# A two-layer decoder trunk: state-space tables with the channel innermost, another order of work around the last gate tile, and two rounds' banks exchanged

## The chip, the cores and the metric

One core of one Trainium2 chip runs the whole program. The metric is the device time of one execution in microseconds. Engines are named as in the profile: PE is TensorE, DVE VectorE, ACT ScalarE, POOL GpSimd, SP SyncE (which issues most transfers).

## The reference

Two layers over 512 tokens of 1024 channels. Each layer has a mixer, then a gated MLP with a causal convolution of width 3, then a gated per-layer embedding. The mixer of layer 0 is gMLP plus attention; that of layer 1 is a diagonal complex state-space layer (S5):

```python
bu_re = jnp.einsum('gpc,bsgc->bsgp', bb_re, uf)   # 64 groups of 16 channels, 64 states each
bu_im = jnp.einsum('gpc,bsgc->bsgp', bb_im, uf)
_, _, xr, xi = lax.associative_scan(_complex_affine_combine, (a_r, a_i, bu_re, bu_im), axis=1)
y = (jnp.einsum('gcp,bsgp->bsgc', c_re, xr) - jnp.einsum('gcp,bsgp->bsgc', c_im, xi) + d * uf)
g_a, g_b = jnp.split(jax.nn.gelu(y) @ od_w_glu, 2, axis=-1)
x = x + g_a * jax.nn.sigmoid(g_b)
# ends every layer:
gate = jax.nn.sigmoid(rms_norm(x) @ ple_w_gate[i])
x = x + gate * (p[i] @ ple_w_proj[i])
```

## The kernel before

Activations lie as 8 tiles of 128 channels x 512 tokens. Every large product is three matmuls (`mm3`): weights and activations are split into a high and a low half (`whi`, `wlo`), `whi` by ACT and `wlo` by DVE (class `Stream`: `prep` makes the halves of one 512 KB chunk, at most up to `limit`; `next` hands out a chunk). The program's order on each engine is the order of the code; small pieces are deferred with `after` (so many steps later) and `next_up`.

**The tables.** While the MLP of layer 0 runs, a generator, `s5_params`, makes the tables of the state-space layer in eight units of eight groups. It is advanced after each weight tile by `background`, which gives it a budget of microseconds per tile: `BG` = `up` for tiles of the up projection, `a` and `b` for the first and the last part of the down projection. A unit computes `ba` and `ca` on DVE (`cmul`, six instructions each), turns `ba` on PE (L1330) into `wv`, copies `bs` into `bd` on ACT (L1337), then multiplies `ca` by `bd` on PE (`kernel`, L1345) and copies `ca` into `wo` (`out_matrix`, L1357). What is left when the last part of the down projection has run seven steps is done at once (`embedding`).

**From the last gate to the first states.** `ple(0)` ends layer 0: eight gate tiles; each is scaled on DVE (L1034), goes through a sigmoid, and `add` puts it into `x[m]` (L1049, L1050). After `add`, `sq_add` squares the tile (ACT) and sums it (POOL, all but the last), and `s5_turn` writes it out turned (`xp`) so that `load_u` can read it as `u`. `state_space` then needs the norm (`rms_sum`, `rms_stat`, with a power on POOL, L213), spread by one small matmul (`scale`, L1486), and multiplies `u` with it (`scaled`, L1493). Eight projections of `p` (`p_proj`, six matmuls each) lie between these steps on PE.

**The state-space rounds.** Four rounds `b`, each of two units: `inputs` (V, L1507), `frame` (DVE and POOL: a rotation, two scans along time, L1522 and L1528, and the rotation back), `states` (four DVE adds into `sg`, L1542), `inside` (the part of a block of eight tokens, L1550, reads `tt`), `outside` (from the states, L1559, reads `wo`), `turn` (transposes), `done` (halves of the result, `ygl`). `part` is the first product of the following GLU. The numbers given to `inputs`, `inside`, `turn` and `bank` are PSUM banks: a step waits until the bank's last reader is through. The tiles `sg0` and `sg1` lie where the halves of `p` lay, so clearing their first column (L1620, POOL) waits for the last `p_proj`.

Of the kernel before, what the change touches and what calls it, by code (L numbers as in the profile page):

```python
# [19 lines left out]
P = 128  # L20
T = 512
# [133 lines left out]
class Kern:  # L155
# [709 lines left out]
    FA, FN, FO = 14, 7, 7  # L865
    BG = {"up": 1.1, "a": 3.3, "b": 2.4}

# [149 lines left out]
    def ple(self, layer, pl):  # L1017
# [11 lines left out]

        def gate(m, ps, c=slice(0, T)):  # L1030
            if c.start == 0:
                gt[m] = pl.tile([P, T], F32, name="gt", tag="gt", bufs=4)
            t = gt[m]
            nc.vector.tensor_tensor(t[:, c], ps[:, c], self.rB[:, c], ALU.mult)  # L1034

            def rest():
                nc.scalar.activation(t[:, c], t[:, c], AF.Sigmoid)
                if m and c.start == 0 and not (layer and m == KT - 1):
                    add(m - 1)
                if m == KT - 1 or (layer and m == KT - 2):  # L1040
                    add(m, c)

            self.post.append(rest)
            if m == KT - 1:
                self.run_post()

        def add(m, c=slice(0, T)):
            t = gt[m]
            nc.vector.tensor_tensor(t[:, c], t[:, c], pp[m][:, c], ALU.mult)  # L1049
            nc.vector.tensor_tensor(self.x[m][:, c], self.x[m][:, c], t[:, c], ALU.add)  # L1050
            if layer == 0:
                self.sq_add(m, self.x[m], m == KT - 1)
                self.s5_turn(m, pl)
            else:
                nc.sync.dma_start(self.out[m][:, c], self.x[m][:, c])
# [177 lines left out]
    def s5_params(self, g5):  # L1233
# [15 lines left out]
        for i in range(8):  # L1249
            q.tensor_copy(apr[:, :, :, i], ap[:, :, 7 - i])  # L1250
        apk = g5.tile([P, 2, 32, 9], F32, name="s5apk", tag="s5apk", bufs=1)
        for i in range(9):
            q.tensor_copy(apk[:, :, :, i], ap[:, :, i])
        v1, v2 = (g5.tile([P, 4, 144], F32, name=f"s5v{i}", tag=f"s5v{i}", bufs=1) for i in range(2))
# [48 lines left out]
        def unit(u):  # L1303
# [14 lines left out]

            ca = g5.tile([P, 2, 4, 16, 9], F32, name="s5ca", tag="s5ca", bufs=1)
            w = [v.rearrange("p a (c k) -> p a c k", c=16) for v in (v1, v2)]  # L1320
            ar, ai = (apk[:, r, g].rearrange("p g (o k) -> p g o k", o=1).to_broadcast([P, 4, 16, 9]) for r in range(2))
            cr, ci = (cc[:, r].rearrange("p g (c o) -> p g c o", o=1).to_broadcast([P, 4, 16, 9]) for r in range(2))
            yield from cmul(ca[:, 0], ca[:, 1], ar, ai, cr, ci, *w, 0.8)
# [16 lines left out]
            def kernel():  # L1340

                ps = self.aux()
                for i in range(4):
                    for r in range(2):
                        nc.tensor.matmul(ps[32 * i:32 * i + 32, 0:P], d[:, r, i],  # L1345
                                         ca[:, r, i, :, 0:8].rearrange("p c k -> p k c"), start=r == 0, stop=r == 1,
                                         tile_position=(0, 32 * i))
# [6 lines left out]
            def out_matrix():  # L1354
                wo = g5.tile([P, 2, 4, 128], F32, name="s5wo", tag="s5wv", bufs=1)
                for r in range(2):
                    nc.scalar.activation(wo[:, r].rearrange("p q (c i) -> p q c i", i=8), ca[:, r, :, :, 1:9], AF.Copy,  # L1357
                                         scale=1.0 - 2 * r)
# [14 lines left out]
    def s5_open(self, g5, s5a):  # L1373
# [3 lines left out]
        self.de = [s5a.tile([P, 8, 64], F32, name=f"de{i}") for i in range(4)]  # L1377
        self.m8 = g5.tile([P, 16, 8], F32, name="m8", tag="s5apk", bufs=1)
        self.nc.gpsimd.tensor_copy(self.m8, self.i8.rearrange("p (o i) -> p o i", o=1).to_broadcast([P, 16, 8]))
# [79 lines left out]
    def state_space(self, s5b):  # L1459
# [53 lines left out]
        def frame(b):  # L1513
# [9 lines left out]
            nc.gpsimd.tensor_tensor(t[5], t[1], si, ALU.mult)  # L1523
            nc.gpsimd.tensor_tensor(t[4], t[1], co, ALU.mult)
            tt(t[2], vi, co, ALU.mult)
# [18 lines left out]
        def inside(b, b0):  # L1544
# [3 lines left out]
            for g in range(8):  # L1548
                for k in range(2):
                    nc.tensor.matmul(Y[b][g // 4][64 * k:64 * k + 64, g % 4 * P:(g % 4 + 1) * P]  # L1550
                                     .rearrange("p (c i) -> p c i", i=8), self.ut[2 * b + k][:, g],
                                     tt[:, 8 * k + g].rearrange("p (i c) -> p c i", c=16), start=g % 4 == 0, stop=False)

        def outside(b):

            y = s5b.tile([P, 2, T], F32, name="y", tag="y", bufs=2)
            for g in range(8):
# [4 lines left out]
                if g % 4 == 3:  # L1562
                    nc.scalar.activation(y[:, g // 4], Y[b][g // 4], AF.Gelu_apprx_tanh)
            Y[b] = y

        def turn(b, b0):

            y = Y.pop(b).rearrange("p z (m i) -> p i (z m)", i=8)
            Z[b] = [bank(b0 + z, "Z") for z in range(2)]
# [34 lines left out]
        self.rms_sum(ps, self.sqa, True, False)  # L1604
        p_proj(w, 3, 7)
        self.rms_sum(ps, self.sql, False, True)
# [16 lines left out]
        p_proj(w, 7, 7)  # L1623
        self.load_in(4)
# [32 lines left out]
        inputs(3, 0, (1,))  # L1657
        frame(2)
        self.ws.dma(self.ws.n_use + 4)
        turn(1, 6)  # L1660
        inside(3, 2)
        done(1)
# [82 lines left out]
```

## Time and profile before

| | before |
|---|---|
| median of 3 runs | 1231.68 us (1229.73 to 1231.99) |
| profiled execution | 1233.72 us, its span 1232.0 us |
| granted PE clock, mean | 0.995 |
| PE / DVE / ACT / POOL busy | 98% / 64% / 43% / 22% |

The span is that of one profiled execution from its first to its last instruction; 1.7 us of its time lie around it. Busy shares are means over all stages. A PE that waits shows as a gap with the engine that ended it.

### The profile page before, as it was taken

Reading aid. Unit: us, or ns where it says so; the run is one execution under the profiler, and the core shown is the slowest. Engines: PE = TensorE matmul, PEld = TensorE weight load, DVE = VectorE, ACT = ScalarE, POOL = GpSimd, SP = SyncE. Lnnn points to the kernel's source line nnn. Section 1 sums busy time; section 2 is a strip of 40 time slices with the busy share of each in tenths; the row PEclk is TensorE's granted clock in tenths of the full one; section 3 lists DMA queues with packets and bytes.
Section 4 is the critical chain, followed back from the end, with each engine's and each line's share of the span. In section 5 each row is a group of like instructions: output and inputs, shape, how many; then the busy total and the mean of one; then the engine's idle time right before and its main releaser. Section 6 shows DMA issues by size and latency. Waiting matters only on the chain.

```text
span 1232.0 us, 15578 instructions
## 1 busy us (share of the span) xinstructions
PE 1208.4 (98%) x5858; PEld 973.0 (79%) x5858; DVE 784.5 (64%) x1156; ACT 531.8 (43%) x796; POOL 271.8 (22%) x453
## 2 busy tenths in 40 slices
PE   9999999999999999998999889999999999999998
PEld 7877678888888778886887678888888888888787
DVE  5597555599777866766545984538956532365545
ACT  5563664355444333444546124325544422234441
POOL 1561335870960221012402110110000000000110
PEclk9999999999999999999999999999999999999999
DMA  6323123233443554324487862332333233331441
GB/s 234 104 86 138 35 68 133 91 112 103 137 134 93 152 153 153 110 81 134 150 237 211 239 241 70 103 114 74 103 103 99 79 100 99 103 98 43 133 154 69
DMA packets 62314, 150.05 MB, mean 122 GB/s; under 512 B 14408, under 2 KB 23880, under 8 KB 62112
## 3 DMA queue, kind: packets, MB, share of 16 engines
q1 hardware_dynamic: 57504, 135.30, 35.5%
q0 software_dynamic: 4160, 12.90, 3.1%
q8 instruction: 46, 0.75, 0.3%
q10 hardware_dynamic: 576, 0.86, 0.2%
q14 instruction: 28, 0.23, 0.1%
HBM read 131.20 MB, written 17.84 MB: 121 GB/s over the span
## 4 chain that ended last, share of the span: by engine, by line
PE 91%; DVE 5%; DMA 1%; ACT 1%; issue 1%; SPq 0%; POOL 0%; ACTq 0%; DVEq 0%; POOLq 0%
PE acc L188 25%; PE acc L190 25%; PE acc L189 25%; PE acc L439 2%; PE acc L441 2%; PE acc L440 2%; PE S L721 1%; PE S L720 1%; PE m L779 1%; PE PT L762 1%; PE aux L1345 1%; PE fil L188 1%; PE fil L190 1%; DVE sg L1542 1%; PE fil L189 1%
## 5 line engine op out<-in xcount | busy, mean ns | idle before, releaser
L140 DVE TENSOR_TENSOR wlo<-raw,whi 128x1024 fp32r<-128x1024 f32 (+3 forms) x207 | 250.8, 1213 | 241.6 <-ACT whi L136 238.1
L136 ACT ACTIVATE whi<-raw 128x1024 fp32r<-128x1024 f32 (+3 forms) x207 | 208.9, 1010 | 358.5 <-PE acc L189 299.6
L188 PE MATMUL acc<-nl,whi 128*128 128x512 f32 x480 | 187.2, 390 | 0.0
L189 PE MATMUL acc<-nh,whi 128*128 128x512 f32 x480 | 186.8, 389 | 0.0
L190 PE MATMUL acc<-nh,wlo 128*128 128x512 f32 x480 | 186.8, 389 | 0.0
L241 POOL TENSOR_TENSOR sqa<-sqa,sqt 128x512 f32<-128x512 f32 x30 | 39.5, 1318 | 497.1 <-ACT sqt L237 497.1
L188 PE MATMUL acc<-xl,whi 128*128 128x512 f32 (+1 forms) x360 | 141.5, 393 | 0.0
L189 PE MATMUL acc<-xh,whi 128*128 128x512 f32 (+1 forms) x360 | 140.8, 391 | 0.0
L190 PE MATMUL acc<-xh,wlo 128*128 128x512 f32 (+1 forms) x360 | 140.8, 391 | 0.0
L188 PE MATMUL acc<-al,whi 128*128 128x512 f32 x352 | 139.8, 397 | 0.9 <-ACT whi L136 0.9
L190 PE MATMUL acc<-ah,wlo 128*128 128x512 f32 x352 | 138.3, 393 | 1.1 <-DVE wlo L140 1.1
L189 PE MATMUL acc<-ah,whi 128*128 128x512 f32 x352 | 138.3, 393 | 0.0
L188 PEld LDWEIGHTS acc<-nl,whi 128*128 128x128 f32 x480 | 90.1, 188 | 19.5 <-ACT whi L136 0.4
L190 PEld LDWEIGHTS acc<-nh,wlo 128*128 128x128 f32 x480 | 90.1, 188 | 18.8
L189 PEld LDWEIGHTS acc<-nh,whi 128*128 128x128 f32 x480 | 90.1, 188 | 18.6
L925 DVE SCALAR_TENSOR_TENSOR cv<-acc,vecs,cv 128x511 f32<-128x511 f32 x120 | 89.4, 745 | 2.1
L188 PEld LDWEIGHTS acc<-al,whi 128*128 128x128 f32 x352 | 66.3, 188 | 18.1 <-issue 2.6
L190 PEld LDWEIGHTS acc<-xh,wlo 128*128 128x128 f32 x360 | 67.8, 188 | 15.8
L189 PEld LDWEIGHTS acc<-xh,whi 128*128 128x128 f32 x360 | 67.8, 188 | 15.5
L188 PEld LDWEIGHTS acc<-xl,whi 128*128 128x128 f32 x360 | 67.8, 188 | 15.4
L190 PEld LDWEIGHTS acc<-ah,wlo 128*128 128x128 f32 x352 | 66.4, 189 | 16.7 <-DVE wlo L140 1.9
L189 PEld LDWEIGHTS acc<-ah,whi 128*128 128x128 f32 x352 | 66.5, 189 | 14.2
(386 smaller groups left out, 1974.5 us busy)
## 6 DMA issues: line engine op xcount, KB each, us to landing
raw<-w_up SPq DMA_DIRECT2D x88, 512.0 KB, 3.5
raw<-w_down SPq DMA_DIRECT2D x26, 512.0 KB, 3.5
raw<-w_in SPq DMA_DIRECT2D x19, 512.0 KB, 3.6
raw<-w_down SPq DMA_DIRECT2D x22, 384.0 KB, 3.1
raw<-w_gate SPq DMA_DIRECT2D x16, 512.0 KB, 3.6
raw<-w_glu SPq DMA_DIRECT2D x16, 512.0 KB, 4.3
x<-xT SPq DMA_DIRECT2D x16, 256.0 KB, 4.6
raw<-w_out SPq DMA_DIRECT2D x8, 512.0 KB, 3.6
```

The source lines that it names most:

```text
L136: k.nc.scalar.activation(hi[:, :n], t[:, :n], AF.Copy)
L140: e.tensor_tensor(lo[:, :n], t[:, :n], hi[:, :n].bitcast(F32), ALU.subtract)
L188: mm(out, whi, xlo, start=start, stop=False)
L189: mm(out, whi, xhi, start=False, stop=False)
L190: mm(out, wlo, xhi, start=False, stop=stop)
L241: (e or (nc.vector if m == KT - 1 else nc.gpsimd)).tensor_tensor(self.sqa, self.sqa, t, ALU.add)
L439: mm(ps[t], xl[:, ts], hi[:, cs], start=k == 0, stop=False)
L440: mm(ps[t], xh[:, ts], hi[:, cs], start=False, stop=False)
L441: mm(ps[t], xh[:, ts], lo[:, cs], start=False, stop=k == KT - 1)
L720: mm(ss[qi][:, 0:n], q[:, qs], k[:, 0:n], start=True, stop=False)
L721: mm(ss[qi][:, 0:n], q[rows, qs], kl[rows, 0:n], start=False, stop=True)
L925: nc.vector.scalar_tensor_tensor(t[:, k:T], h[:, 0:T - k], w[2 - k], t[:, k:T], ALU.mult, ALU.add)
```

## The change

1. `ca` is built as (k, c) instead of (c, k), straight from `ap`; the copy `apk` goes. The `kernel` matmul, the matmul of `inside` and the transposes then read along memory; `wo`, and the result tile `y`, have the token of the block outside and the channel inside.
2. The budgets of the generator: `up` from 1.1 to 1.3, `a` from 3.3 to 3.4.
3. In layer 0 `add(6)` is called ahead of the last gate's scaling, and tile 6's turned copy behind tile 7's square.
4. In `state_space` the two sums of the norm stand together, `p_proj(3)` behind them, `scale` at once behind that, `inputs(0)` behind `p_proj(4)`, `p_proj(7)` behind `inside(0)`. Weight chunks of the GLU are prepared only after `scaled(4..7)`.
5. In `frame`, one of the two POOL products goes to DVE.
6. The banks of `inputs(2)` and `inside(2)` change places, and so on for round 3; `inside(2)` and `turn(0)` go ahead of `inputs(2)`, and `inputs(3)` is no longer in two pieces.

```diff
-    BG = {"up": 1.1, "a": 3.3, "b": 2.4}
+    BG = {"up": 1.3, "a": 3.4, "b": 2.4}
...
+            last = layer == 0 and m == KT - 1
...
+            if last:
+                add(m - 1)
             t = gt[m]
             nc.vector.tensor_tensor(t[:, c], ps[:, c], self.rB[:, c], ALU.mult)
...
-                if m and c.start == 0 and not (layer and m == KT - 1):
+                if 0 < m < KT - 1 and c.start == 0:
                     add(m - 1)
...
+                if m == KT - 1:
+                    self.s5_turn(m - 1, pl)
                 self.sq_add(m, self.x[m], m == KT - 1)
-                self.s5_turn(m, pl)
+                if m != KT - 2:
+                    self.s5_turn(m, pl)
...
-            ca = g5.tile([P, 2, 4, 16, 9], F32, name="s5ca", tag="s5ca", bufs=1)
...
-            ar, ai = (apk[:, r, g].rearrange("p g (o k) -> p g o k", o=1).to_broadcast([P, 4, 16, 9]) for r in range(2))
-            cr, ci = (cc[:, r].rearrange("p g (c o) -> p g c o", o=1).to_broadcast([P, 4, 16, 9]) for r in range(2))
+            ca = g5.tile([P, 2, 4, 9, 16], F32, name="s5ca", tag="s5ca", bufs=1)
...
+            ar, ai = (ap[:, r, :, g].rearrange("p k (g o) -> p g k o", o=1).to_broadcast([P, 4, 9, 16]) for r in range(2))
+            cr, ci = (cc[:, r].rearrange("p g (o c) -> p g o c", o=1).to_broadcast([P, 4, 9, 16]) for r in range(2))
...
-                                         ca[:, r, i, :, 0:8].rearrange("p c k -> p k c"), start=r == 0, stop=r == 1,
+                                         ca[:, r, i, 0:8].rearrange("p k c -> p (k c)"), start=r == 0, stop=r == 1,
...
             nc.gpsimd.tensor_tensor(t[5], t[1], si, ALU.mult)
-            nc.gpsimd.tensor_tensor(t[4], t[1], co, ALU.mult)
...
             tt(t[2], t[3], co, ALU.mult)
+            tt(t[4], t[1], co, ALU.mult)
...
-                    nc.tensor.matmul(Y[b][g // 4][64 * k:64 * k + 64, g % 4 * P:(g % 4 + 1) * P]
-                                     .rearrange("p (c i) -> p c i", i=8), self.ut[2 * b + k][:, g],
-                                     tt[:, 8 * k + g].rearrange("p (i c) -> p c i", c=16), start=g % 4 == 0, stop=False)
+                    nc.tensor.matmul(Y[b][g // 4][64 * k:64 * k + 64, g % 4 * P:(g % 4 + 1) * P],
+                                     self.ut[2 * b + k][:, g], tt[:, 8 * k + g], start=g % 4 == 0, stop=False)
...
-                    nc.scalar.activation(y[:, g // 4], Y[b][g // 4], AF.Gelu_apprx_tanh)
+                    nc.scalar.activation(y5[:, g // 4], Y[b][g // 4].rearrange("p (g i c) -> p g i c", g=4, i=8),
+                                         AF.Gelu_apprx_tanh)
...
+        self.ws.limit = self.ws.n_use + 2
         w = self.ws.next()
...
         self.rms_sum(ps, self.sqa, True, False)
-        p_proj(w, 3, 7)
         self.rms_sum(ps, self.sql, False, True)
...
+        p_proj(w, 3, 7)
+        rt = scale()
         w = self.ws.next()
         p_proj(w, 4, 0)
-        p_proj(w, 5, 1)
-        rt = scale()
+        inputs(0, 2)
...
+        p_proj(w, 5, 1)
         p_proj(w, 6, 6)
-        inputs(0, 2)
-        p_proj(w, 7, 7)
...
+        self.ws.limit = None
+        self.ws.prep(self.ws.n_use + 1)
         inside(0, 0)
         self.load_kernel(2)
+        p_proj(w, 7, 7)
         inputs(1, 4)
...
-        inputs(2, 2)
+        inside(2, 2)
         turn(0, 0)
         done(0)
         states(1)
-        inside(2, 4)
...
-        inputs(3, 0, (0,))
+        inputs(2, 4)
+        inputs(3, 0)
         outside(1)
```

The order on three engines, where it moves. First ACT near the end of layer 0's MLP: `whi` are weight halves, `cv` and `ah` belong to the MLP, `xh`, `sqa` and `sqt` to its finished tiles, the `s5` names to the last unit of the tables. Before:

```order
L136 ACTIVATE whi<-raw 128x256
L206 ACTIVATE xh_5081<-x_112 128x512
L234 ACTIVATE sqa<-x_112 128x512
L136 ACTIVATE whi<-raw 128x1024
L206 ACTIVATE xh_5083<-x_113 128x512
L237 ACTIVATE sqt<-x_113 128x512
L136 ACTIVATE whi<-raw 128x1024
L206 ACTIVATE xh_5085<-x_114 128x512
L237 ACTIVATE sqt<-x_114 128x512
L136 ACTIVATE whi<-raw 128x1024
L1331 ACTIVATE s5wv<-aux 128x512 x2
L1337 ACTIVATE s5bd_3509<-s5bs 64x4x16 x4
```

The same unit on ACT after the change:

```order
L928 ACTIVATE cv<-cv 128x512
L1334 ACTIVATE s5wv<-aux 128x512 x2
L1340 ACTIVATE s5bd_3423<-s5bs 64x4x16 x4
L136 ACTIVATE whi<-raw 128x256
L940 ACTIVATE ah_5030<-cv 128x512
L136 ACTIVATE whi<-raw 128x256 x2
L1352 ACTIVATE s5kp_3425<-aux 128x112
L1360 ACTIVATE s5wo<-s5ca 128x512 x2
L206 ACTIVATE xh_5109<-x_112 128x512
```

The last unit's copies now stand ahead of the residual's tiles, with weight halves between `s5bd` and `s5kp`, where before they stood behind three of them.

Second, DVE around the last gate tile (`gt` is the gate, `rB` the norm, `pp6` and `pp7` the embeddings of tiles 6 and 7). Before:

```order
L1050 TENSOR_TENSOR x5_117<-x5_117,gt_5770 128x512
L1034 TENSOR_TENSOR gt_5850<-acc_5825,rB_5526 128x512
L1049 TENSOR_TENSOR gt_5810<-gt_5810,pp6_5398 128x512
L1050 TENSOR_TENSOR x6_118<-x6_118,gt_5810 128x512
L1049 TENSOR_TENSOR gt_5850<-gt_5850,pp7_5399 128x512
L1050 TENSOR_TENSOR x7_119<-x7_119,gt_5850 128x512
L140 TENSOR_TENSOR wlo_5874<-raw_5673,whi_5873 128x1024
L254 TENSOR_SCALAR rc_5922<-aux_5904 128x4
```

And after:

```order
L1053 TENSOR_TENSOR x5_117<-x5_117,gt_5760 128x512
L1052 TENSOR_TENSOR gt_5800<-gt_5800,pp6_5388 128x512
L1053 TENSOR_TENSOR x6_118<-x6_118,gt_5800 128x512
L1037 TENSOR_TENSOR gt_5840<-acc_5815,rB_5516 128x512
L1052 TENSOR_TENSOR gt_5840<-gt_5840,pp7_5389 128x512
L1053 TENSOR_TENSOR x7_119<-x7_119,gt_5840 128x512
L254 TENSOR_SCALAR rc_5899<-aux_5890 128x4
```

Tile 6's sum moved ahead of the last gate's scaling, and the weight half moved away (it stands behind `scaled(7)`, ahead of `frame(1)`).

Third, POOL from the norm to the second round's frame (`st` are the frame's tiles). Before:

```order
L213 TENSOR_TENSOR rc_5922<-rc_5922,mhalf_142 128x4
L1620 MEMSET sg0_5871 128x16
L1620 MEMSET sg1_5872 128x16
L1523 TENSOR_TENSOR st5_6026<-st1_6022,tab_5519 128x512
L1524 TENSOR_TENSOR st4_6025<-st1_6022,tab_5519 128x512
L1523 TENSOR_TENSOR st5_6171<-st1_6167,tab_6019 128x512
```

And after:

```order
L213 TENSOR_TENSOR rc_5899<-rc_5899,mhalf_142 128x4
L1625 MEMSET sg0_5861 128x16
L1625 MEMSET sg1_5862 128x16
L1526 TENSOR_TENSOR st5_6003<-st1_5999,tab_5509 128x512
L1526 TENSOR_TENSOR st5_6161<-st1_6157,tab_5996 128x512
```

Each frame has one product less on POOL; the clearing of `sg` still stands in front of the first one. On SP nothing changes its place.

## Rows read from the trace of the kernel before

**Rows 1.** The first section of the page: busy microseconds, share of the span, instructions.

```profile
PE 1208.4 (98%) x5858; PEld 973.0 (79%) x5858; DVE 784.5 (64%) x1156; ACT 531.8 (43%) x796; POOL 271.8 (22%) x453
```

**Rows 2.** Who TensorE waited for: total us, times, longest us.

```profile
PE Y L1559 <- DVE sg L1542: 3.9, 5, 1.9
PE aux L1345 <- ACT s5bd L1337: 3.7, 1, 3.7
PE Y L1550 <- DVE st L1526: 2.2, 1, 2.2
```

**Rows 3.** Busy time of each engine in five stretches (length, then busy us and instructions of PE, PEld, DVE, ACT, POOL; then the granted clock as a share of full speed, the DMA share and GB/s).

```profile
392.00:480.00 88.00, 88.00 (x456) 69.18 (x455) 63.65 (x90) 32.54 (x62) 20.63 (x34) 1.00 0.50 149
580.50:584.00 3.50, 0.09 (x1) 0.09 (x2) 2.17 (x2) 3.46 (x8) 1.52 (x2) 1.00 0.37 138
584.40:587.80 3.40, 3.40 (x20) 2.41 (x20) 0.83 (x2) 0.27 (x2) 0.57 (x1) 0.51 0.86 275
682.00:735.20 53.20, 43.72 (x493) 34.58 (x492) 51.90 (x67) 11.57 (x17) 11.87 (x8) 0.96 0.81 259
734.60:738.00 3.40, 3.31 (x30) 2.91 (x32) 1.79 (x2) 0.60 (x1) 0.00 (x0) 0.50 0.10 30
```

**Rows 4.** Groups of instructions by line and shape: count, then busy us and mean ns of one, then idle time before them.

```profile
L1259 DVE TENSOR_TENSOR s5v<-s5apk,s5cc 128x576 f32<-128x576 f32 x16 | 12.1, 754 | 0.2
L1345 PE MATMUL aux<-s5ca,s5bd 128*32 128x128 f32 x128 | 9.6, 408 | 3.7 <-ACT s5bd L1337 3.7
L1528 DVE TENSOR_TENSOR_SCAN st<-de,st 128x512 f32<-128x512 f32 x4 | 8.8, 2188 | 0.1
L1523 POOL TENSOR_TENSOR st<-st,tab 128x512 f32<-128x512 f32 x4 | 5.1, 1279 | 35.3 <-DVE st L1522 23.2 <-issue 12.1
L1522 DVE TENSOR_TENSOR_SCAN st<-de,st 128x512 f32<-128x512 f32 x4 | 4.9, 1225 | 0.1
L1259 DVE TENSOR_TENSOR s5v<-s5co,s5bb 128x512 f32<-128x512 f32 x2 | 1.4, 686 | 0.1
```

**Rows 5.** TensorE in the order of time, at the tables' matmuls and at the small weight pieces of the down projection, of layer 0 (574) and of layer 1 (1153): start, length, instruction, count, and in brackets the idle time before it with its releaser.

```profile
398.61 1.13 PE L1345 MATMUL aux<-s5ca,s5bd 128*32 128x128 f32 x16
399.68 0.50 PE L188 MATMUL acc<-al,whi 128*128 128x512 f32 x1
...
573.65 0.50 PE L188 MATMUL acc<-al,whi 128*128 128x512 f32 x1 [0.69 <-ACT whi L136]
574.90 0.50 PE L190 MATMUL acc<-ah,wlo 128*128 128x512 f32 x1 [0.53 <-DVE wlo L140]
583.91 1.70 PE L1345 MATMUL aux<-s5ca,s5bd 128*32 128x128 f32 x16 [3.71 <-ACT s5bd L1337]
...
1152.82 0.50 PE L188 MATMUL acc<-al,whi 128*128 128x512 f32 x1 [0.19 <-ACT whi L136]
...
1154.08 0.50 PE L190 MATMUL acc<-ah,wlo 128*128 128x512 f32 x1 [0.53 <-DVE wlo L140]
```

**Rows 6.** TensorE in the order of time in the state-space part.

```profile
673.01 0.95 PE L245 MATMUL aux<-onesd,sqt 128*128 128x1 f32 x8
676.63 0.33 PE L1486 MATMUL rt<-rj,m 128*128 128x64 f32 x2
678.34 2.08 PE L1507 MATMUL V<-u,wv 128*64 128x64 f32 x64
681.95 3.69 PE L1550 MATMUL Y<-tt,u 128*64 128x128 f32 x32
721.02 1.97 PE L1559 MATMUL Y<-wo,sg 128*64 128x128 f32 x32
734.50 3.82 PE L1559 MATMUL Y<-wo,sg 128*64 128x128 f32 x32 [1.88 <-DVE sg L1542]
```

**Rows 7.** VectorE in the order of time, from the last gate tile to the last states.

```profile
665.91 0.69 DVE L1034 TENSOR_TENSOR gt<-acc,rB 128x512 f32<-128x512 f32 x1 [1.22 <-PE acc L190]
672.47 1.23 DVE L140 TENSOR_TENSOR wlo<-raw,whi 128x1024 fp32r<-128x1024 f32 x1 [3.01 <-ACT whi L136]
674.00 0.16 DVE L254 TENSOR_SCALAR rc<-aux 128x4 f32<-128x4 f32 x1 [0.31 <-PE aux L245]
675.29 0.23 DVE L1483 TENSOR_TENSOR rj<-rc,s5j 128x64 f32<-128x64 f32 x1 [1.13 <-POOL rc L213]
677.26 2.50 DVE L1493 TENSOR_TENSOR u<-u,rj 128x512 f32<-128x512 f32 x4
680.36 0.69 DVE L1519 TENSOR_TENSOR st<-V,tab 128x512 f32<-128x512 f32 x1 [0.60 <-PE V L1507]
685.58 2.18 DVE L1528 TENSOR_TENSOR_SCAN st<-de,st 128x512 f32<-128x512 f32 x1
688.40 0.68 DVE L1530 TENSOR_TENSOR st<-st,tab 128x512 f32<-128x512 f32 x1
732.37 2.79 DVE L1542 TENSOR_TENSOR sg<-st,st 64x504 f32<-64x504 f32 x4
```

**Rows 8.** GpSimd in the order of time, at the first frame.

```profile
681.39 0.19 POOL L1620 MEMSET sg<- 128x16 f32 x2 [6.13 <-PE pk L190]
683.71 1.28 POOL L1523 TENSOR_TENSOR st<-st,tab 128x512 f32<-128x512 f32 x1 [2.13 <-DVE st L1522]
684.95 1.73 POOL L1524 TENSOR_TENSOR st<-st,tab 128x512 f32<-128x512 f32 x1
```

More of the change, by code (lines that the diff above doesn't have):

```diff
@@ L1250, in s5_params @@
             q.tensor_copy(apr[:, :, :, i], ap[:, :, 7 - i])
-        apk = g5.tile([P, 2, 32, 9], F32, name="s5apk", tag="s5apk", bufs=1)
-        for i in range(9):
-            q.tensor_copy(apk[:, :, :, i], ap[:, :, i])
         v1, v2 = (g5.tile([P, 4, 144], F32, name=f"s5v{i}", tag=f"s5v{i}", bufs=1) for i in range(2))
@@ L1317, in unit @@
                 yield 0.2
-            ca = g5.tile([P, 2, 4, 16, 9], F32, name="s5ca", tag="s5ca", bufs=1)
-            w = [v.rearrange("p a (c k) -> p a c k", c=16) for v in (v1, v2)]
-            ar, ai = (apk[:, r, g].rearrange("p g (o k) -> p g o k", o=1).to_broadcast([P, 4, 16, 9]) for r in range(2))
-            cr, ci = (cc[:, r].rearrange("p g (c o) -> p g c o", o=1).to_broadcast([P, 4, 16, 9]) for r in range(2))
+            ca = g5.tile([P, 2, 4, 9, 16], F32, name="s5ca", tag="s5ca", bufs=1)
+            w = [v.rearrange("p a (k c) -> p a k c", c=16) for v in (v1, v2)]
+            ar, ai = (ap[:, r, :, g].rearrange("p k (g o) -> p g k o", o=1).to_broadcast([P, 4, 9, 16]) for r in range(2))
+            cr, ci = (cc[:, r].rearrange("p g (o c) -> p g o c", o=1).to_broadcast([P, 4, 9, 16]) for r in range(2))
             yield from cmul(ca[:, 0], ca[:, 1], ar, ai, cr, ci, *w, 0.8)
@@ L1356, in out_matrix @@
                 for r in range(2):
-                    nc.scalar.activation(wo[:, r].rearrange("p q (c i) -> p q c i", i=8), ca[:, r, :, :, 1:9], AF.Copy,
+                    nc.scalar.activation(wo[:, r].rearrange("p q (i c) -> p q i c", i=8), ca[:, r, :, 1:9], AF.Copy,
                                          scale=1.0 - 2 * r)
@@ L1377, in s5_open @@
         self.de = [s5a.tile([P, 8, 64], F32, name=f"de{i}") for i in range(4)]
-        self.m8 = g5.tile([P, 16, 8], F32, name="m8", tag="s5apk", bufs=1)
+        self.m8 = s5a.tile([P, 16, 8], F32, name="m8")
         self.nc.gpsimd.tensor_copy(self.m8, self.i8.rearrange("p (o i) -> p o i", o=1).to_broadcast([P, 16, 8]))
@@ L1549, in inside @@
                 for k in range(2):
-                    nc.tensor.matmul(Y[b][g // 4][64 * k:64 * k + 64, g % 4 * P:(g % 4 + 1) * P]
-                                     .rearrange("p (c i) -> p c i", i=8), self.ut[2 * b + k][:, g],
-                                     tt[:, 8 * k + g].rearrange("p (i c) -> p c i", c=16), start=g % 4 == 0, stop=False)
+                    nc.tensor.matmul(Y[b][g // 4][64 * k:64 * k + 64, g % 4 * P:(g % 4 + 1) * P],
+                                     self.ut[2 * b + k][:, g], tt[:, 8 * k + g], start=g % 4 == 0, stop=False)
         def outside(b):
-            y = s5b.tile([P, 2, T], F32, name="y", tag="y", bufs=2)
+            y = s5b.tile([P, 8, P], F32, name="y", tag="y", bufs=2)
+            y5 = y.rearrange("p i (z g c) -> p z g i c", z=2, g=4)
             for g in range(8):
@@ L1562, in outside @@
                 if g % 4 == 3:
-                    nc.scalar.activation(y[:, g // 4], Y[b][g // 4], AF.Gelu_apprx_tanh)
+                    nc.scalar.activation(y5[:, g // 4], Y[b][g // 4].rearrange("p (g i c) -> p g i c", g=4, i=8),
+                                         AF.Gelu_apprx_tanh)
             Y[b] = y
         def turn(b, b0):
-            y = Y.pop(b).rearrange("p z (m i) -> p i (z m)", i=8)
+            y = Y.pop(b)
             Z[b] = [bank(b0 + z, "Z") for z in range(2)]
@@ L1656, in state_space @@
         self.load_out(5)
-        inputs(3, 0, (1,))
         frame(2)
@@ L1660, in state_space @@
         turn(1, 6)
-        inside(3, 2)
+        inside(3, 4)
         done(1)
@@ L1676, in state_space @@
         part(w, 6, 1, 2, 4)
-        turn(2, 4)
+        turn(2, 2)
         done(2)
@@ L1684, in state_space @@
         outside(3)
-        acc[4], acc[5] = bank(4, "acc"), bank(5, "acc")
+        acc[4], acc[5] = bank(2, "acc"), bank(3, "acc")
         w = self.ws.next()
         part(w, 0, 4, 0, 4)
-        turn(3, 2)
+        turn(3, 4)
         done(3)
@@ L1698, in state_space @@
         part(w, 6, 1, 6, 8)
-        self.rings(acc=(2, 3, 6, 7, 0, 1, 4, 5), aux=(2, 3))
+        self.rings(acc=(4, 5, 6, 7, 0, 1, 2, 3), aux=(4, 5))
         self.new_xh()
```

## The prediction, made before the changed kernel had run

> **What bounds the kernel now.** I read first the busy times: PE works 1208 of 1232 us [rows 1], so a gain must either shorten what PE does or remove one of its waits. The list of waits [rows 2] then names the places: `sg` and `st` from VectorE in the state-space part, and one single wait of 3.7 us for `s5bd` in the tables. The windows [rows 3] tell how the two places differ. From 392 to 480, where the tables are made, PE is busy 88.00 of 88.00 us and VectorE 63.65: PE bounds, and whatever a table matmul costs is in the time. From 682 to 735.2 it is the other way round: VectorE is busy 51.90 of 53.20 us, PE only 43.72. There the chain of `frame`, `states` and `done` on VectorE bounds, and PE's 9.5 us of idle time are its shadow. A faster matmul in that stretch gives only a longer wait.
>
> **The sum, part by part.** It is made on the profiled execution, 1233.72 us; the median, 1231.68, is 2.0 lower, and the same gains are taken from it.
>
> *Contiguous reading in the tables (gain 3.8).* `kernel` reads `ca` with a step of nine elements. Sixteen records take the slot from 398.61 to 399.68, 1.07 us [rows 5]. No row shows the same shape read along memory. The nearest pair is in the state-space part: 32 records of `inside`, which step by sixteen elements, take 3.69 us, 32 of `outside`, of the same rows and columns but contiguous, 1.97 [rows 6], a ratio of 0.53. At this ratio a slot is 0.57 us and eight units save 8 x 0.5 = 4.0; since the start of the next matmul does not shrink I take 0.47 each, 3.8. Bounds: 0 (the step isn't the cause) and 4.0.
>
> *The tables end earlier (gain 5.9).* Before, the eighth unit is unfinished when `embedding` empties the generator: turning, the copies into `s5bd` and `kernel` follow each other at once, behind three weight halves on ScalarE's queue, and PE waits 3.71 us [rows 5]. With the budgets 1.3 and 3.4 the order shows the unit's copies ahead of the residual's tiles, and `kernel` some 50 matmuls behind its transposes; so the wait goes: 3.7. After it the clock was granted at 0.51, the 1.2 GHz level, for 3.4 us in which PE was busy throughout; in the 3.5 us ahead of that PE had worked 0.09 us [rows 3]. Without the wait I expect the 2.4 GHz level: half of 3.4, 1.7. Lastly the waits of 0.69 and 0.53 at the small weight pieces [rows 5] came behind table products on VectorE; the same pieces of layer 1, with no tables, wait 0.19 and 0.53. The table products are gone from there: 0.5. What is late next here is nothing that the trace shows. The cost: VectorE gets 0.2 us more per up tile of about 5.5 us, hidden under its idle share (24.35 of 88 us from 392 to 480); uncovered it would cost what VectorE lacks. The nine copies into `apk` on POOL go; nothing waited for them, so 0.
>
> *The new operand order on VectorE and ScalarE (0).* `ca`'s products now repeat one operand over the inner sixteen elements and read the other along memory. That form exists: 686 ns for 512 elements against 754 for 576 now [rows 4], both 1.3 ns an element. Bounds 0 and, if it went wrong, the rival below. The GELU writes `y` in runs of sixteen; I take 0, because between it and its reader VectorE's chain is late anyway. The transposes gain nothing, they stand in that shadow too.
>
> *The first frame starts earlier (gain 3.3).* Now `frame(0)` starts at 680.36, when V is ready [rows 7]. Step by step for the changed order: tile 6's sum uses the 1.22 us in which VectorE waited for the last gate [rows 7], so tile 7's square is ready before PE has done the first sums at about 670.9. The second sums, now directly behind them, end at about 671.8; before they ended at 673.96 [rows 6], so the norm is at 671.9 instead of 674.00. From there to the end of the small product on VectorE it is 1.5 us (674.00 to 675.52), 673.4; `p_proj(3)` on PE lasts till about 673.2 and is hidden. `scale`'s matmul, before held till 676.63 behind two projections [rows 6], runs at 673.4 (0.3); the copy and two of the four `scaled` take till 675.3. PE does `p_proj(4)` meanwhile, till 675.1, then `inputs(0)`, 2.0 us: V at 677.1. So 3.3. Bounds 2.0 (one more projection in the way) and 3.6. The other projections now fill PE behind it, in the shadow.
>
> *A product from POOL to VectorE (gain 1.4).* The second scan takes 2.18 us, the first 1.22 [rows 4]; the second one runs beside POOL's L1524 [rows 7, 8]. With that product gone the scan should take 1.22: 0.96 less, against one more product on VectorE, 0.61 from start to start. 0.35 in each of four frames. Bounds 0 and 1.4.
>
> *The first weight half of the GLU (loss 1.1).* Before, its `wlo` of 1.23 us ran at 672.47, where VectorE had been idle for 3 us [rows 7]. Now it stands between `scaled(7)` and `frame(1)`, in the chain: 1.23 less the 0.1 by which neighbours overlap.
>
> *POOL's remaining product in the first frame (loss 1.1).* The clearing of `sg0` waits for the last projection, and the product is queued behind it [rows 8]. Before, the projection was over in time. Now `p_proj(7)` stands behind `inside(0)`: 677.1 plus two projections (2.9) and `inside(0)` (1.9) gives 681.9, and its reads of `sg0`'s place end near 682.8. The first scan ends already at 680.4. So the product starts near 683.1 instead of 680.5, beside the second scan and the products behind it. Where the two met before, the scan lost 0.96 us [rows 4]; the product itself lasts 1.28. I take 1.1; bounds 0 and 1.3. The Trainium skill says of this (SBUF — State Buffer, Who interferes with whom) that a VectorE instruction with two inputs in SBUF and a GpSimd instruction that reads SBUF exclude each other, and that whichever starts first holds the other up entirely. By it the product waits for the scan and then holds the next VectorE product for its whole 1.28 us; the sum would be 0.2 us longer. Rows 4, 7 and 8 agree with it.
>
> *Banks and order of the rounds (0).* `inside(2)` no longer waits for `frame(1)`'s PSUM reads (2.2 us [rows 2]), but `inputs(2)` now does, and `inputs(3)` still waits for `done(0)`. PE's idle time moves; the chain stays. On SP the table of round 1 now follows `p_proj(7)`, a microsecond later than against `frame(0)`, with the kernel tables of round 2 behind it; they are wanted only under the same shadow.
>
> State-space part: -3.3 - 1.4 + 1.1 + 1.1 = -2.5: the last `sg`, written till 735.16 [rows 7], comes 2.5 earlier, and PE is full behind it. Tables: -3.8 - 5.9 = -9.7. Together -12.2: 1221.5 for the profiled execution and **1219.5** for the median.
>
> **The rivals.**
> - *The end at full clock.* The wait of 1.88 before the last `outside` is followed by 3.4 us at clock 0.50 [rows 3, 6], again the 1.2 GHz level, on PE's own path. PE waits about as long after the change, so I leave it; if it is spared, 1.7 more: 1217.8. The 0.5 clock may as well come later and cost the same.
> - *The state-space part gives nothing:* the early start is eaten by POOL's product and the weight half, or PE becomes late for V. For it: VectorE gains only 0.35 a frame. Against: each step above has 2 us of room on PE. 1222.0.
> - *The step isn't the cause* of the slow table matmul (the change does not do what it says): 1223.3. Against: `inside` and `outside` differ in nothing else that the rows show.
> - *The wait for `s5bd` stays,* with its clock: 1219.5 + 5.4 = 1224.9. Against it stands the order.
> - *Slower: VectorE pays for the new order of `ca`.* From 392 to 480 five units make 30 of the 48 products. VectorE's idle 24.35 us there allow each 0.81 us more, 1.57 instead of 0.75. From there PE waits: each 0.1 us costs 3.0. At 2.05 us the gain of 12.2 is gone with 2.5 on top: about 1234. The row of 686 ns speaks against it.
>
> **How the numbers follow.** Forecast 0.55; end at full clock 0.15; nothing in the state-space part 0.14; step not the cause 0.05; wait stays 0.05; VectorE pays 0.03; else 0.03. Within 0.2% (2.5 us, about what three runs with a spread of 2.3 us can tell apart) lies only a part of the last two. Faster 0.96, same 0.01, slower 0.03. The range reaches from the end at full clock without POOL's loss (1216.7) past the first rivals to the wait that stays: 1216 to 1224.5. The forecast's own range, from its bounds, is 1217.5 to 1222.
>
> **What would show it.** Table matmuls of about 0.6 us a slot; no wait for `s5bd` and no half clock near 575; `inside` near 2.0 us but more PE idle time in the state-space part; `frame(0)` about 3 us nearer to the last gate; second scans of 1.22 except perhaps in the first frame, where a VectorE instruction stretches by about 1 us; VectorE still 95% busy there. Wrong it would be made by `s5ca` products above 0.8 us, by waits of PE for `whi` or `wlo` in the tables' stretch, or by a chain through PE in the state-space part.

## The result, and the profile after

| | before | after |
|---|---|---|
| median, us (runs) | 1230.98 (4; 1229.73 to 1231.99) | 1219.64 (4; 1219.48 to 1220.99) |
| ratio of the times | | 0.9911, 95% interval 0.9894 to 0.9928 |
| profiled execution, us | 1233.72 | 1219.66 |

The forecast was 1219.5 in 1216 to 1224.5. The busy times answer [rows 1]: PE is busy 14.6 us less (1208.4 to 1193.8), VectorE as much as before.

```profile
span 1217.7 us, 15570 instructions
PE 1193.8 (98%) x5858; PEld 965.4 (79%) x5858; DVE 784.8 (64%) x1160; ACT 531.3 (44%) x796; POOL 260.2 (21%) x440
```

PE's waits, longest first (total us, times, longest), against [rows 2]: `s5bd` is gone, a transfer (`wv`) is new near the top, and the waits for `ygl` have grown from 1.9 us in all to 5.3.

```profile
PE Y L1562 <- DVE sg L1545: 3.2, 4, 1.5
PE Y L1553 <- DMA wv<-wvd: 3.1, 1, 3.1
PE V L1510 <- DVE ygl L1591: 2.7, 2, 2.5
PE acc L188 <- DVE ygl L1591: 2.6, 1, 2.6
```

Stretches of the kernel after (columns as in [rows 3]). The state-space part now lies 14.5 us earlier, so 667.5 to 720.7 answers 682 to 735.2.

```profile
392.00:480.00 88.00, 88.00 (x455) 71.07 (x454) 67.21 (x94) 32.95 (x63) 21.54 (x35) 1.00 0.51 154
574.00:580.00 6.00, 6.00 (x28) 4.95 (x28) 3.82 (x6) 3.13 (x5) 1.30 (x1) 1.00 0.37 103
667.50:720.70 53.20, 38.94 (x504) 32.45 (x502) 51.98 (x71) 13.27 (x20) 5.47 (x6) 0.97 0.84 258
721.30:724.70 3.40, 3.40 (x26) 2.78 (x21) 0.57 (x1) 1.94 (x3) 0.00 (x0) 0.51 0.47 143
```

PE has still no idle time from 392 to 480, behind the tables the clock stays at 1.00, and VectorE is as full in the state-space part as before (51.98 of 53.20), while PE's busy time there fell from 43.72 to 38.94: what PE got faster, it waits longer. The last row is the half clock behind the last `outside`, which is still there.

TensorE after, in order of time (the eighth unit's table matmul, the small weight pieces, the norm to V, the first `inside`, the new wait, the last `outside`):

```profile
563.41 0.66 PE L1348 MATMUL aux<-s5ca,s5bd 128*32 128x128 f32 x16
564.00 0.51 PE L188 MATMUL acc<-al,whi 128*128 128x512 f32 x1
...
568.59 0.50 PE L188 MATMUL acc<-al,whi 128*128 128x512 f32 x1 [0.17 <-ACT whi L136]
...
661.46 0.43 PE L1489 MATMUL rt<-rj,m 128*128 128x64 f32 x2
...
663.25 2.09 PE L1510 MATMUL V<-u,wv 128*64 128x64 f32 x64
...
668.22 1.97 PE L1553 MATMUL Y<-tt,u 128*64 128x128 f32 x32
...
682.29 1.97 PE L1553 MATMUL Y<-tt,u 128*64 128x128 f32 x32 [3.14 <-DMA wv<-wvd]
...
719.96 0.44 PE L1562 MATMUL Y<-wo,sg 128*64 128x128 f32 x4 [1.52 <-DVE sg L1545]
```

VectorE from the norm to the second frame, and the last `sg`:

```profile
659.89 0.16 DVE L254 TENSOR_SCALAR rc<-aux 128x4 f32<-128x4 f32 x1 [1.89 <-PE aux L245]
...
665.27 0.69 DVE L1522 TENSOR_TENSOR st<-V,tab 128x512 f32<-128x512 f32 x1 [0.58 <-PE V L1510]
...
670.48 1.22 DVE L1530 TENSOR_TENSOR_SCAN st<-de,st 128x512 f32<-128x512 f32 x1
671.74 1.59 DVE L1531 TENSOR_TENSOR st<-st,tab 128x512 f32<-128x512 f32 x1
673.25 0.68 DVE L1532 TENSOR_TENSOR st<-st,tab 128x512 f32<-128x512 f32 x1
...
679.80 1.22 DVE L140 TENSOR_TENSOR wlo<-raw,whi 128x1024 fp32r<-128x1024 f32 x1
680.94 0.68 DVE L1522 TENSOR_TENSOR st<-V,tab 128x512 f32<-128x512 f32 x1
...
717.82 2.79 DVE L1545 TENSOR_TENSOR sg<-st,st 64x504 f32<-64x504 f32 x4
```

GpSimd at the first frame, and the groups that answer [rows 4]:

```profile
671.14 0.19 POOL L1625 MEMSET sg<- 128x16 f32 x2 [9.99 <-PE pk L190]
671.32 1.46 POOL L1526 TENSOR_TENSOR st<-st,tab 128x512 f32<-128x512 f32 x1
```

```profile
L1262 DVE TENSOR_TENSOR s5v<-s5ap,s5cc 128x576 f32<-128x576 f32 x16 | 12.1, 754 | 0.2
L1348 PE MATMUL aux<-s5ca,s5bd 128*32 128x128 f32 x128 | 5.3, 279 | 0.0
L1530 DVE TENSOR_TENSOR_SCAN st<-de,st 128x512 f32<-128x512 f32 x4 | 4.9, 1224 | 0.1
```

**Where the time went.** The start of one and the same weight matmul in both traces gives the gain up to that place. It is 2.07 us at 100 us, 11.82 at 600, still 11.82 ahead of the last gate's projections, and 14.30 from 740 to the end. So three places gained: the start of the program 2.1, the tables 9.74, the state-space part 2.48; everywhere else nothing. No line at the start was changed. There the first matmuls of the profiled execution of before stood 0.43 us apart until about 11 us, where those after stand 0.235 apart:

```profile
6.90 0.63 PE L440 MATMUL acc<-whi,xh 128*128 128x512 f32 x1
7.33 0.63 PE L441 MATMUL acc<-wlo,xh 128*128 128x512 f32 x1
```

```profile
7.67 0.40 PE L441 MATMUL acc<-wlo,xh 128*128 128x512 f32 x1
7.90 0.40 PE L439 MATMUL acc<-whi,xl 128*128 128x512 f32 x1
```

The clock column reads 1.00 there in both, but only because it has nothing to read: the trace of before holds no record of the clock ahead of 11.0 us, that of after none ahead of 4.5. In each profile that begins slowly the first record, at full clock, starts within 0.15 us of where the slow pace ends, and 0.43 us is also the distance of such matmuls at the recorded clock of 0.51 (before, 586.1 to 587.4 us). So the start most likely ran at the 1.2 GHz level too; the traces can't show it directly.

The profiles of the experiments below begin at either pace, although only the last two change the start (slow: pace undone, step, head undone, half early, half in gap, banks undone). Their effects are therefore given place by place from the traces (the shift of the same matmul, less its shift at 300 us), and their medians beside it (before: 1230.94 to 1231.72 over the three groups of runs).

### The profile page after: what moved, and what is told of

Its sections match the earlier page's. It is cut to its first block, busy times and chain, and to the rows that moved or that the text cites. A ratio compares the mean times of both kernels' runs of the same rounds, so it can differ in the third digit from the quotient of the medians.

```text
span 1217.7 us, 15570 instructions
## 1 busy us (share of the span) xinstructions
PE 1193.8 (98%) x5858; PEld 965.4 (79%) x5858; DVE 784.8 (64%) x1160; ACT 531.3 (44%) x796; POOL 260.2 (21%) x440
```

## The experiments

**The tables: pace and step.** Three kernels.

```
 after:   BG = {"up": 1.3, "a": 3.4, ...}  ->  {"up": 1.1, "a": 3.3, ...}         pace undone
 before:  BG = {"up": 1.1, "a": 3.3, ...}  ->  {"up": 1.3, "a": 3.4, ...}         pace alone
 after:   ca[:, r, i, 0:8].rearrange("p k c -> p (k c)")  ->  (... "p k c -> p c k")
          tt[:, 8 * k + g]  ->  tt[:, 8 * k + g].rearrange("p (i c) -> p c i", c=16)    step
```

> The changed kernel with the old budgets of the tables' generator (1.1 and 3.3). Theory (the pace is what removed the wait): the eighth unit is left over for `embedding` again, PE waits about 3.7 us for `s5bd`, 3.4 us at half clock follow it (1.7), and the small weight pieces ahead of it wait 0.5 longer: 5.9 us more than the changed kernel, about 1225.5. Rival (the shorter slots alone brought the units forward): no wait over 0.7 us near 575, about 1219.6. The slots of the table matmuls stay at 0.6 us under both.

> The kernel before with nothing but the new budgets (1.3 and 3.4). Theory: the wait for `s5bd`, its half-clock stretch and 0.5 us of the small waits go, 5.9 us less than before, about 1225.1; slots stay at 1.06 us. Rival (the wait needs the new layout too, because strided units take longer): the wait stays at least at 2 us, 1228 or more.

> The changed kernel, but the moving operand of the tables' `kernel` and of `inside` is read with a step of 16 elements again, from the same tiles (the columns then come in another order, so the tables and Y are permuted: this run is for its time alone). Theory (the step is the cause, and `inside` lies in VectorE's shadow): table slots 1.06 us instead of 0.60, 8 x 0.47 = 3.8 us more; `inside` 3.7 us instead of 1.97 with nothing to the end of the last `sg`; about 1223.4. Rival 1 (layout in memory, not the step of the reading, is the cause): slots stay at 0.6, 1219.6. Rival 2 (PE is near to the path in the state-space part): each `inside` costs up to 1.7 us there, up to 1230.

Pace undone: 1225.91 us, tables 6.05 longer than after. Pace alone: 1225.98 (ratio to before 0.9952, 0.9935 to 0.9969), tables 6.07 shorter than before. The wait and the half pace behind it are back in the first of them, with the contiguous layout:

```profile
580.22 1.64 PE L1348 MATMUL aux<-s5ca,s5bd 128*32 128x128 f32 x16 [3.72 <-ACT s5bd L1340]
581.79 0.80 PE L188 MATMUL acc<-al,whi 128*128 128x512 f32 x1
```

The pace alone makes and removes the wait; the layout has no part in it. Step: 1223.48, tables 3.39 longer (a slot takes 1.02 to 1.03 us with this step of 16 values, 1.06 with before's step of 9, 0.60 after), `inside` at 3.70 again, and the table matmuls (group of this kernel) at

```profile
L1348 PE MATMUL aux<-s5ca,s5bd 128*32 128x128 f32 x128 | 8.8, 398 | 0.0
```

against 5.3 above, from the same tiles in the same memory: it is the step of the reading. The Trainium skill (SBUF — State Buffer, Door 1: The DMA port swizzle) has a note that consecutive accesses should stay within one 16-byte line, four fp32 values, and that each further line costs; the runs agree in sign for steps of 9 and 16 values, and the note gives no size. The step also shows that `inside` was not wholly in the shadow. The first one, 1.7 us longer, holds `p_proj(7)` and with it the clearing of `sg` and GpSimd's product, for which `sg` now waits (VectorE, step kernel):

```profile
679.79 2.79 DVE L1545 TENSOR_TENSOR sg<-st,st 64x504 f32<-64x504 f32 x4 [1.17 <-POOL st L1526]
```

Since the product behind the scan is back at 0.69 there, 0.27 us of it is left at the last `sg`.

**The way to the first frame.** The old order as a whole, then the first weight half in two other places.

```
 head undone:   p_proj(w, 3, 7) between the two rms_sum; p_proj 4 and 5 ahead of scale();
                p_proj 6, inputs(0, 2), p_proj 7 ahead of frame(0); gate tail as before
 half early:    - self.ws.limit = self.ws.n_use + 2
                - self.ws.limit = None;  self.ws.prep(self.ws.n_use + 1)
 half in gap:     self.s5_turn(m - 1, pl)
                + self.ws.prep(self.ws.n_prep + 1)        (in add, last tile)
                  self.ws.limit = self.ws.n_use + 2  ->  + 3
```

> The changed kernel with the old order between the last gate tile and the first frame (old gate tail; `p_proj(3)` between the sums, `p_proj(4)` and `(5)` ahead of `scale`, `p_proj(6)` ahead of `inputs(0)`, `p_proj(7)` right behind it); the weight half stays in VectorE's chain, the products as after. Theory: `frame(0)` starts 3.3 us later against the last gate; POOL's clearing of `sg0` is no longer held, so the first frame gets back the 0.9 us by which its first product behind the scan was stretched: net 2.4 us more than the changed kernel, about 1222.0. Rival (the first frame is not on the path): 0 or less, 1219.6.

> The changed kernel without the two edits of `ws.limit`, so that the third weight chunk's halves are made as early as before. Theory A (the limit is what keeps the short way short): `whi` stands behind the turned copy of tile 7 on ScalarE, 659.74 to 660.8, and its `wlo` ahead of the norm's copy on VectorE: the norm comes at about 662.0 instead of 659.9, `frame(0)` 2.1 us later, the 1.1 in the chain is won back: 1.0 more, 1220.6. Theory B (the place in idle time is free, as it was before the change): 1.1 less, 1218.5.

> The changed kernel with the same chunk's halves put between the copies of tiles 6 and 7: `whi` on ScalarE from 656.9 to 657.9, where it waits for tile 7, and `wlo` on VectorE from about 658.0 to 659.25, ahead of the norm's copy at 659.89, where VectorE waits for the sums. Theory: `frame(0)` stays, `frame(1)` comes 1.13 us nearer to it, 1218.5. Rival (ScalarE's square of tile 7 or a weight that has not landed delays the norm): `frame(0)` later by up to 1 us, 1219.5.

The times of the table are counted from the first matmul of the eight projections (665.71 in the trace of before, 653.89 after).

| from the first projection, us | `frame(0)` starts | last `sg` ends | median |
|---|---|---|---|
| before | 14.65 | 69.45 | 1230.98 |
| after | 11.38 | 66.72 | 1219.64 |
| head undone | 14.71 | 69.16 | 1222.12 |
| half early | 14.88 | 69.35 | 1221.67 |
| half in gap | 11.38 | 65.59 | 1218.66 |

The head undone costs 2.44 at the last `sg`, as the theory had it (3.3 less 0.9). The half in the gap gives 1.13, the whole of its price. The half early is worse than expected, 2.6 instead of 1.0: the norm comes 2.0 later as reckoned, but `frame(0)` 3.5 later. PE waited 2.10 us for the norm, and soon after the clock was granted at 0.50, the 1.2 GHz level, from 665.3 to 668.7 us. The projection's matmuls stood 0.43 us apart there and V came late; VectorE waited 2.12 for it (VectorE, then that stretch, columns as in [rows 3]):

```profile
662.25 1.22 DVE L140 TENSOR_TENSOR wlo<-raw,whi 128x1024 fp32r<-128x1024 f32 x1 [2.72 <-ACT whi L136]
663.39 0.15 DVE L254 TENSOR_SCALAR rc<-aux 128x4 f32<-128x4 f32 x1
...
670.30 0.69 DVE L1522 TENSOR_TENSOR st<-V,tab 128x512 f32<-128x512 f32 x1 [2.12 <-PE V L1510]
...
665.30:668.70 3.40, 3.40 (x21) 2.37 (x22) 2.72 (x5) 0.60 (x1) 0.00 (x0) 0.50 0.28 64
```

**GpSimd's product.** Both products on GpSimd again; `p_proj(7)` moved ahead; the clearing moved behind.

```
 two on POOL:   + nc.gpsimd.tensor_tensor(t[4], t[1], co, ALU.mult)      (behind the one for t[5])
                - tt(t[4], t[1], co, ALU.mult)
 p_proj early:    p_proj(w, 7, 7) ahead of inside(0, 0)
 clear late:      the two memsets of sg between frame(0) and states(0)
```

> The changed kernel with both products of `frame` on GpSimd again. Theory: the second scan takes 2.18 us in the last three frames and the product of 0.61 goes, 0.35 more each, 1.05; in the first frame both products start at 671.3 and lie beside the products behind the scan and the first `sg`, which waits for them: 2 x 1.3 from 671.7 is 674.3, against 674.57 now, so -0.3 to +0.9; in all 0.8 to 2.0 more, about 1220.9. Rival (the scan's lengthening is not due to GpSimd's product): scans of 1.22, 2.4 us less.

> The changed kernel with `p_proj(7)` ahead of `inside(0)` instead of behind `load_kernel(2)`. Theory (POOL's product in the first frame is held by the clearing of `sg0`, which waits for this projection): the projection ends near 669.9 instead of 671.76, the product then runs beside the second scan's forerunners, the product of 1.59 us behind the scan is 0.69 again: the last `sg` 0.9 us nearer to `frame(0)`, 1218.7. Rival A (wherever POOL's product lands, VectorE pays the same): 0, 1219.6. Rival B (`inside(0)`, 1.7 us later, now delays the first `outside`): up to 0.5 more.

> The changed kernel with the clearing of the two `sg` tiles behind the first frame's product on GpSimd instead of ahead of it. Theory (GpSimd's product costs VectorE time only beside products of two SBUF tiles; beside the two that read V in PSUM it costs nothing, as in the last three frames): the product starts when the first scan ends, all products of the first frame are 0.68 to 0.75 again, the first `sg` ends 0.85 us nearer to `frame(0)`; about 1218.7. Rival (the product costs its 0.3 to 0.9 us wherever it lands in this frame, as in the run with `p_proj(7)` moved): at most 0.3 us.

Two on POOL: 1221.41 us, the last `sg` 1.71 later: 0.37 in each of the last three frames, whose second scans take 2.19 again, and 0.59 in the first. There GpSimd was held until the scan was over, and the products behind it were stretched instead, to 1.58 and 1.77. `p_proj` early: 1218.53, but only 0.28 of the 0.9 was won at the last `sg`: the product now fell on the subtraction of two SBUF tiles ahead of the scan. Clear late: 1217.36, and the product fell on the two that read V in PSUM. VectorE and GpSimd with `p_proj` early:

```profile
668.86 0.68 DVE L1528 TENSOR_TENSOR st<-V,tab 128x512 f32<-128x512 f32 x1
669.57 1.29 DVE L1529 TENSOR_TENSOR st<-st,st 128x512 f32<-128x512 f32 x1
...
669.03 1.29 POOL L1526 TENSOR_TENSOR st<-st,tab 128x512 f32<-128x512 f32 x1
```

and with the clearing late:

```profile
668.49 0.67 DVE L1527 TENSOR_TENSOR st<-V,tab 128x512 f32<-128x512 f32 x1
669.07 0.68 DVE L1528 TENSOR_TENSOR st<-V,tab 128x512 f32<-128x512 f32 x1
669.79 0.75 DVE L1529 TENSOR_TENSOR st<-st,st 128x512 f32<-128x512 f32 x1
...
668.71 1.29 POOL L1526 TENSOR_TENSOR st<-st,tab 128x512 f32<-128x512 f32 x1 [7.54 <-PE pk L190]
```

The first frame is 0.83 us shorter by that, as expected. Of it 0.59 is left at the last `sg`; 0.23 went between `frame(1)` and `frame(2)`, with the same wait and the same half clock as in the last experiment below (PE waits 4.92 us, and the clock is 0.51 from 681.2 to 688.1). Of the 2.3 us between the medians another 1.6 goes with the half clock at the end, which this profile does not have; that this is an effect of the edit is not shown. The Trainium skill (SBUF — State Buffer, Who interferes with whom) says that a VectorE instruction with at most one input in SBUF, outside the modes that use two ports, does not contend with GpSimd: 0.67 and 0.68 beside the product, 0.66 and 0.68 without it, agree.

**Banks and order of the rounds.**

```
 - inside(2, 2) ... inputs(2, 4); inputs(3, 0); outside(1)
 + inputs(2, 2) ... inside(2, 4); inputs(3, 0, (0,)); outside(1); inputs(3, 0, (1,))    (and the old banks)
```

> The changed kernel with the old banks and the old order of the second and third round (`inputs(2)` ahead of the turn, `inside(2)` behind the states, `inputs(3)` in two halves). Theory (all of this lies in VectorE's shadow): the chain from `frame(0)` to the last `sg` stays at 55.3 us, 1219.6. Rival (the exchange keeps PE from being late for V): a frame waits for V, 0.5 to 2 us more.

1220.38 us; from `frame(0)` to the last `sg` 55.29 against 55.34: nothing, as expected. Its profile began at the slow pace (1.2 us), which is more than the 0.7 between the medians.

**The clock, and all together.**

```
 fill:  + ps = bank(2, "fill");  6 x nc.tensor.matmul(ps[:, 0:P], self.ident, self.ident)   ahead of outside(3)
          for _ in range(8)  ->  range(11)                                       (at the program's start)
 all:     clear late + half in gap + fill
```

> The changed kernel with six small matmuls without a reader in PE's wait ahead of the last `outside`, and eleven instead of eight at the start of the program. Theory (the half-clock stretches follow PE's waits): no half clock near 721 in the profile, 1.6 us less there than in the changed kernel's profile; first matmuls at full pace in every run, so the times lie within 0.6 us of each other; median 1217.9. Rival (the stretch comes from the earlier waits at 702 and 712, or by chance): the stretch at 721 stays or moves, 1219.6 with the same spread of 1.5 to 2 us.

> The changed kernel with the late clearing, the weight half in the gap ahead of the norm's copy, and the filled waits together. Theory: the sum of the single runs, -0.85 for the product, -1.13 for the weight half, -1.6 for the clock at the end: about 1216.0, 3.6 us under the changed kernel. Rival (the chain through VectorE is shorter and PE becomes late for V or for a transfer, since it had to wait for `wv` at 682): 1217 to 1218.

Fill: 1218.25 us, and its four times lie within 0.32 (1217.97 to 1218.29). PE before the last `outside` of this kernel, and the weight matmuls behind it at full pace:

```profile
718.54 1.50 PE L1692 MATMUL fill<-ident 128*128 128x128 f32 x12
720.22 0.44 PE L1562 MATMUL Y<-wo,sg 128*64 128x128 f32 x4 [0.18 <-DVE sg L1545]
...
722.95 0.40 PE L189 MATMUL acc<-ygh,whi 128*128 128x512 f32 x1
```

At the end 1.6 us were spared. That the fill did it is not shown: of the twelve profiles without it, six (before, after, pace alone, step, two on POOL, banks undone) had the half clock behind the last `outside`, and six (pace undone, head undone, half early, half in gap, `p_proj` early, clear late) had none. The length of the wait ahead of it does not decide it alone: it is 1.9 us in before, pace alone and two on POOL, and 1.5 in the other nine, of which three had the half clock. Something else goes with it: all six without it had a stretch of half clock 17 to 28 us earlier, beginning between 699 and 707 us, and of the six with it only before and two on POOL had one near there. The profile of fill has such a stretch too, from 703.1 to 706.5, so it looks like those that were spared without any fill. What decides between them stays open. The differences given above end at the last `sg` and don't hold these 1.6 us.

All together: 1217.38 (1216.89 to 1217.67), ratio to before 0.9892 (0.9877 to 0.9907): 2.3 below after, not the 3.6 of the sum, and no better than the late clearing alone (1217.36). The rival came out, in its number and in the late transfer; a half clock came with it. `frame(1)` comes 1.98 nearer to `frame(0)`, but `frame(2)` 1.43 later behind `frame(1)`. `inside(2)`, which now stands ahead of the turn, waits 4.99 us on PE for the kernel table of round 2 (`tt`); the clock is 0.50 from 682.0 to 688.3, the turn's result comes late, and VectorE's `done(0)` waits 1.33 for it:

```profile
683.35 3.68 PE L1554 MATMUL Y<-tt,u 128*64 128x128 f32 x32 [4.99 <-DMA wv<-wvd]
686.96 1.71 PE L1576 MATMUL Z<-ident,y 128*128 128x128 f32 x8
688.75 1.29 DVE L1592 TENSOR_TENSOR ygl<-Z,ygh 128x512 fp32r<-128x512 f32 x2 [1.33 <-ACT ygh L1591]
```

```profile
682.00:688.30 6.30, 4.95 (x39) 4.65 (x40) 5.31 (x8) 0.18 (x1) 1.27 (x1) 0.50 1.06 343
```

(The profile names the transfer last on the queue, `wv`; the eight pieces of `tt` were issued ahead of it.) SP issued them from 672.21 on. `inside(0)` had freed their buffer at 670.2, but ahead of them on SP stands the table of `frame(1)`, `tab`, and that waits for `p_proj(7)` (SP's own waits, 664 to 690 us):

```profile
SPq L1392 <- PE pk L190: 5.3, 1, 5.3
```

The late table alone doesn't explain the loss. In half in gap `inside(2)` starts at 683.35 as well, after a wait of 2.72, but at full clock: it and the turn are over at 686.3, 2.3 us earlier than here, and `done(0)` doesn't wait. Here VectorE was free for `done(0)` at 687.4, so at full clock the turn would have been in time (an estimate from these numbers). Whether the long wait brought the half clock is not shown; the two profiles with such a wait, this one and clear late, both have it. The old order of the second round, which turns and makes V first, would not stand behind this table, and with `p_proj(7)` early the pieces were issued from 671.40; neither was run with the other three edits.

## Why the prediction was right, by its own steps

| term | forecast, us | measured in the traces |
|---|---|---|
| table matmuls, contiguous | -3.8 | -3.7: the 9.74 of the tables less the 6.07 of the pace alone; group 9.6 [rows 4] to 5.3, 0.6 of it from the half clock of the eighth |
| wait for `s5bd` | -3.7 | -3.71 |
| half clock behind it | -1.7 | -1.8, what is left of the 6.07 beside the wait and the weight pieces |
| small weight pieces | -0.5 | -0.52 (0.69 to 0.17; the other stays 0.53) |
| new operand order of `ca` | 0 | 0 (754 ns before and after) |
| `frame(0)` earlier | -3.3 | -3.27 |
| product to VectorE | -1.4 | -1.5: 0.36 in each of the last three frames (after against before), 0.45 in the first (head undone against before) |
| weight half in the chain | +1.1 | +1.13 (half in gap) |
| GpSimd's product in frame 0 | +1.1 | +0.9 |
| banks and order | 0 | 0 (banks undone) |
| sum | -12.2 | -12.2: tables -9.74, state-space part -2.48 (-2.73 at the last `sg`; 0.25 goes again behind the last `outside`) |

- *What bounds.* It held: each step on PE's path in the tables came out in full, and of the 6.9 us by which the four `inside` got faster, 0.27 at most is in the time. That was the one hole in "a faster matmul in that stretch gives only a longer wait": the first `inside` holds the last projection, and through it GpSimd and SP's queue.
- *GpSimd's product* came when it was forecast, 6.05 us behind the start of `frame(0)` (forecast 6.0), but the scan, which had begun first, kept its 1.22 us, and the product behind it was stretched. The prediction left open which instruction would be stretched and took its price from the scan's 0.96 us; the second reading it gave, that the product waits for the scan and then holds the next one, named the right instruction, with 1.28 us for the price. Measured was 0.9, near the 1.1 that was taken.
- *The end at full clock* was given 0.15. In the profile after the half clock was still there; over the twelve kernels it is there in six profiles and missing in six, also under equal waits of 1.5 us. Nothing shows that the change decides it, so it stands as an uncertainty of 1.6 us in each profile.
- *Banks and order* came out at nothing in the changed kernel, where all of it lies in the shadow; in clear late and in all together it no longer does, and the hold of SP behind `p_proj(7)`, which the prediction saw and put at 0, is the first part of the loss there.
- *The step that failed* is the way from the profiled execution to the median. I took it as a constant 2.0; it was 2.7 before and 0.0 after. The sum led to 1221.5 for the profiled execution, which took 1219.66: the start of the program, 2.1 us of the profiled execution of before, was not in the sum. From median to median the gain was 11.3 (interval 8.9 to 13.0). That the forecast median is off by 0.1 is therefore partly luck; the terms are not. One slip among the rivals changes nothing: by its own figures VectorE paying 2.05 us a product leaves 2.2 us on top of the gain, not 2.5.

## What to carry to other kernels

Read first which engine a stretch depends on: on PE's path every faster read and every wait removed came out whole and with the half clock that followed the wait; on VectorE's path only what stands between two VectorE instructions counts. A helper engine's product is free beside instructions that read PSUM and dear beside those that read two SBUF tiles, so what decides is when it starts, and an innocent clearing queued ahead of it can set that. Gains of one chain add up only until the next wait, here for a late transfer, and whatever clock follows it: put together, the three edits gave 2.3 us of the 3.6 expected.

## What was not expected of the hardware

- The first matmuls run at half their pace (0.43 us apart) until 9.6 to 11.1 us in seven of the twelve profiles with the same start of the program, which then takes 1.2 to 2.1 us longer. The clock column can't show it: the trace's first record of the clock comes where the slow pace ends, and a stretch without a record reads 1.00. With eleven instead of eight small matmuls ahead of them, both profiles began at full pace (within 0.25 us), and the four times of each of the two kernels lie within 0.3 and 0.8 us, where the others spread 0.3 to 2.4. That speaks for the three matmuls, but five of the twelve began at full pace without them.
- A wait of 1.5 to 1.9 us ahead of the last `outside` was followed by 3.4 us at clock 0.50 in six profiles; in six others, with 1.5, it was not.
- GpSimd's product holds VectorE's instruction on two SBUF tiles, or is held by it, whichever began first (1.59 for 0.69; 2.19 for 1.22), and passes by those that read PSUM (0.67).
